# Two of the four block sums of each down unit made by adding transfers instead of VectorE

## The chip, the cores and the metric

The kernel runs on one core of a Trainium2 chip. The metric is device time in microseconds (us). It was run three times; the median is 1215.81 us, the lowest 1213.68 us and the highest 1215.82 us. The profiled execution is a run of its own. The five engines of the core have their own in-order queues: TensorE (PE in the profile), VectorE (DVE), ScalarE (ACT), GpSimd (POOL) and SyncE (SP). They wait for each other through semaphores only. Transfers between DRAM and the on-chip memory are issued from the queues of SP, ACT or POOL and then run beside the engines.

## The reference, cut to what matters

The program is one step of a two-layer decoder on 512 prompt rows and 64 sample rows, 576 in all, with a model width of 1024. Each layer has a mixer and an MLP. The change touches the MLP's second product alone:

```python
def sqrelu_mlp(h, w_up, w_down):
    return jnp.square(jax.nn.relu(h @ w_up)) @ w_down      # w_up 1024 x 4096, w_down 4096 x 1024

for l in range(DEPTH):                                     # 2 layers
    ...mixer...
    hp = hp + sqrelu_mlp(rmsnorm(hp, norm_mlp[l]), mlp_w_up[l], mlp_w_down[l])
    hs = hs + sqrelu_mlp(rmsnorm(hs, norm_mlp[l]), mlp_w_up[l], mlp_w_down[l])
```

All of it is in 32-bit floats.

## The kernel before, in words

**Exactness by splitting.** TensorE is used with a shorter float format. Each operand is therefore split in two: a high half (ScalarE copies it into the short format, `whi` for weights, line 272) and a low half (VectorE subtracts the high half from the original, `wlo`, line 283). A product is three passes: high by high, low activations by high weights, high activations by low weights. A pass cannot start before its half has been made.

**The MLP in rounds.** An MLP has four rounds (`rounds_of`), so the two layers have eight. A round makes eight pieces of the hidden layer (the up part, 384 matmuls of line 328 in a row on the chain) and then the part of the down product that these pieces feed. That down part has four units (`down_unit`, m = 0 to 3). A unit takes a 2 x 2 arrangement of weight blocks and a 2 x 2 arrangement of activation blocks and makes the product with seven block products instead of eight, by the scheme of Winograd and Strassen. The price is sums of blocks. The weight blocks are called a11, a12, a21, a22, each 128 x 512 floats (256 KB). The four sums of weights are s1 = a21 + a22, s2 = s1 + a11, s3 = a21 + a11, s4 = s2 + a12 (the signs are in the data's layout and in the additions to the result). The products use them so:

```python
SOURCE = {"P1": "a11", "P2": "a12", "P4": "a22", "P5": "s1", "P6": "s2", "P7": "s3", "P3": "s4"}
UNIT = ("P1", "P5", "P6", "P2", "P7", "P3", "P4")          # order on TensorE, units m = 1 to 3
FIRST_UNIT = ("P1", "P2", "P3", "P5", "P6", "P4", "P7")    # unit m = 0
```

A unit is 84 matmuls, and its results are added to the rows `h` by VectorE (`to_h`, line 547). The last unit of the last round is left as an ordinary product (`last_unit`), so there are 31 units.

**Loads.** `order` is the list of all weight tiles in the order of use, and `load_to` issues a load of 512 KB for each from SP into a buffer `raw`. A down unit takes two of them: the first holds a11 and a12, the second a21 and a22. There are three `raw` buffers. One more, the spare, serves the second tile of units 1 and 3. It shares its memory (tag `q`) with the tile `q` of the activations, so its load for unit 1 has to wait until the last activation sum of the round has been read out of `q`, which is the second subtraction of line 499 (`alo`).

**Order of the work.** In the MLP the order of VectorE and ScalarE is exactly the order in which the program's lines run (a manual schedule). `ahead_to(n)` prepares weights up to n jobs ahead. Before each of them it looks two jobs further and, by the table `SUMS`, issues the sum that belongs to the job, through `total` (line 257). So sums stand on VectorE's queue some places ahead of the halves that need them, and whatever a sum waits for, all later VectorE work waits for too. The order on SP and POOL is left to the scheduler of the language. POOL does nothing in the down parts.

Of the kernel before, what the change touches and what calls it, by code (L numbers as in the profile page):

```python
# [11 lines left out]
F32 = mybir.dt.float32  # L12
F32R = mybir.dt.float32r
AF = mybir.ActivationFunctionType
ALU = mybir.AluOpType
# [3 lines left out]
P = 128  # L19
# [92 lines left out]
COL = {"mix0": 0, "mlp0": 8, "mix1": 16, "mlp1": 24, "fin": 32, "b_o": 40, "b_qkv": 48, "sink_s": 58}  # L112
NCOL = 59
UNIT = ("P1", "P5", "P6", "P2", "P7", "P3", "P4")
SUMS = {"P1": "s1", "P5": "s2", "P2": "s3", "P6": "s4"}
FIRST_UNIT = ("P1", "P2", "P3", "P5", "P6", "P4", "P7")


# [1 line left out]
def hybrid_step(ctx: ExitStack, tc: tile.TileContext, a, o):  # L120
    nc = tc.nc
# [34 lines left out]
    for c in range(KC):  # L156
# [3 lines left out]
        if c % 2 == 0:  # L160
            raw = wp.tile([P, 512], F32, name="rawf", tag="raw", bufs=3)
# [20 lines left out]
    order = [V[1], Q[0], K[1], Q[1], V[2], K[2], Q[2], V[3], K[3], Q[3], *GV, *G, *U]  # L182
# [6 lines left out]
    def add_pieces(aps):  # L189
        for ap in aps:  # L190
            jobs.extend([("left", len(order)), ("right", len(order))])
            order.append(ap)

    def add_unit(pair, first):
        jobs.extend((n, len(order)) for n in (FIRST_UNIT if first else UNIT))
        order.extend(pair)

    def mlp_order(l, last):
        up, dn = a[f"w_up{l}"], a[f"w_dn{l}"]
        for r in range(32 // FB):  # L200
            add_pieces([up[r * FB + f] for f in range(FB)])
            for m in range(KC // 2):
                if last and r == 32 // FB - 1 and m == KC // 2 - 1:
                    add_pieces([dn[r, m, i] for i in range(2)])
                    continue
                add_unit([dn[r, m, i] for i in range(2)], m == 0)
                if m % 2:
                    spare.append(len(order) - 1)
# [6 lines left out]
    raws, parts, owed, spare_open = [], [], [], [False]  # L215
    used, done, summed = [0], [0], [0]
    sums, sum_pool = {}, [None]
# [5 lines left out]
    def load_to(n):  # L223
        while len(raws) < min(n, len(order)):
            if len(raws) in spare:
                raw = sum_pool[0].tile([P, 1024], F32, name="raw", tag="q", bufs=1)
            else:
                raw = wp.tile([P, 1024], F32, name="raw", tag="raw", bufs=3)
            nc.sync.dma_start(out=raw, in_=order[len(raws)].rearrange("p k c -> p (k c)"))
            raws.append(raw)  # L230

    def load_free():

        while len(raws) < len(order):
            n = len(raws)
            if n in spare:
                free = spare_open[0] and all(i < done[0] for i in spare if i < n)
            else:
                same = [i for i in range(n) if i not in spare]
                free = len(same) < 3 or same[-3] < done[0]  # L240
            if not free:
                break
            load_to(n + 1)

    def blocks_of(i):
        load_to(i + 2)
        return {"a11": raws[i][:, 0:512], "a12": raws[i][:, 512:1024],
                "a21": raws[i + 1][:, 0:512], "a22": raws[i + 1][:, 512:1024]}

    def total(k, i):  # L250

        if (k, i) not in sums:
            b = blocks_of(i)
            x, y = {"s1": ("a21", "a22"), "s2": ("s1", "a11"), "s3": ("a21", "a11"), "s4": ("s2", "a12")}[k]
            x = b[x] if x in b else total(x, i)
            sums[k, i] = sum_pool[0].tile([P, 512], F32, name=k, tag="sum", bufs=4)
            nc.vector.tensor_tensor(out=sums[k, i], in0=x, in1=b[y], op=ALU.add)  # L257
        return sums[k, i]
# [3 lines left out]
    def prepare():  # L262

        n, i = jobs[len(parts)]
        if n in ("left", "right"):
            load_to(i + 1)
            src = raws[i][:, 0:512] if n == "left" else raws[i][:, 512:1024]
        else:
            src = blocks_of(i).get(SOURCE[n])
            src = total(SOURCE[n], i) if src is None else src  # L270
        hi, lo = (wp.tile([P, 512], F32R, name=t, tag=t, bufs=NW_) for t in ("whi", "wlo"))
        nc.scalar.copy(out=hi, in_=src)  # L272
        owed.append((src, hi, lo, n, i))
        parts.append((hi, lo))
# [5 lines left out]
    def split_low(n=1):  # L280
        for _ in range(min(n, len(owed))):
            src, hi, lo, n_, i = owed.pop(0)
            nc.vector.tensor_tensor(out=lo, in0=src, in1=hi.bitcast(F32), op=ALU.subtract)  # L283
            if n_ == "P2":

                total("s4", i)
                total("s3", i)
            if n_ in ("right", "P2", "P4"):
                done[0] = i + (2 if n_ == "P4" else 1)

    def split_to(n):
        while len(parts) < min(n, len(jobs)):
            prepare()
            split_low(len(owed))

    def ahead_to(n):

        n = min(n, len(jobs))
        while len(parts) < n or owed:
            while summed[0] < min(len(parts) + 2, len(jobs)):  # L300
                job, i = jobs[summed[0]]
                k = SUMS.get(job)
                if k:
                    total(k, i)
                summed[0] += 1
            if len(parts) < n:
                prepare()
            split_low()
        load_free()
# [367 lines left out]
    def mixer0(norm, nxt):  # L677
        with tc.tile_pool(name="mx0", bufs=2) as mp:
# [31 lines left out]

            split_high(4)
            split_low(2)
            xs = norm.xs
            cosr, sinr = w("cosr"), w("sinr")
# [692 lines left out]
```

## Time and profile before

| | |
|---|---|
| time of the profiled execution | 1217.04 us |
| its span | 1215.2 us (granted TensorE clock 0.994) |
| median of three runs | 1215.81 us |
| TensorE busy | 1190.1 us, 98% of the span |
| VectorE busy | 869.1 us, 72% |
| ScalarE busy | 576.8 us, 47% |
| GpSimd busy | 156.1 us, 13% |
| read from DRAM | 102.92 MB |

Between the span and the time of the execution lie 1.84 us. A row of the profile's groups reads: line, engine, operation, output<-input, partitions x elements, type, count | busy us, mean ns of one | idle time of the engine ahead of it and what ended it. A row of the chain of waits reads: start in us from the span's start, length in us, what the chain passed through (a DMA, an engine's instruction, or "issue", in which the profile shows no wait). A row of the timeline has start, length from the start of the first to the end of the last, engine, line, operation, operands, shape, count and, in brackets, the idle time before and what ended it. Lines are those of the kernel before.

### The profile page before, as it was taken

To read this page: it belongs to the slowest core of one execution; us is meant where nothing else is said; L and a number is where in the kernel's file an instruction comes from. 1 tells how busy PE (TensorE), PEld (TensorE's weight loads), DVE (VectorE), ACT (ScalarE), POOL (GpSimd) and SP (SyncE) were. 2 spreads that over 40 slices of the span, in tenths; PEclk is the share of its full clock that TensorE was granted. 3 is DMA by queue.
4 is the path that set the end of the run, shared out by engine and by line. 5 is a ranking of instruction groups with operands and counts; after the bars stand their busy time and mean duration, and the time that the engine had idled before them with its cause. 6 is when DMAs were issued, how large, how long until landed. Compare 5 with 4: busy or idle time off the path is not lost.

```text
span 1215.2 us, 22586 instructions
## 1 busy us (share of the span) xinstructions
PE 1190.1 (98%) x9177; PEld 1172.4 (96%) x9177; DVE 869.1 (72%) x1608; ACT 576.8 (47%) x1084; POOL 156.1 (13%) x137
## 2 busy tenths in 40 slices
PE   8999999999999999999999999999999999999996
PEld 8998999999999999999999989999999999999996
DVE  8967685447865875785796768646794795695696
ACT  6333554344443544453465777535453553453452
POOL 3443250110000000000001654120000000000000
PEclk9999999999999999999999999999999999999998
DMA  7244222222232232232223212122223132232222
GB/s 271 104 140 120 78 71 74 85 70 87 88 105 71 84 118 72 73 108 85 86 86 111 70 38 70 36 87 70 83 92 105 52 122 86 72 105 87 76 81 79
DMA packets 38263, 109.42 MB, mean 90 GB/s; under 512 B 4160, under 2 KB 12544, under 8 KB 38144
## 3 DMA queue, kind: packets, MB, share of 16 engines
q1 hardware_dynamic: 37440, 107.36, 28.7%
q8 instruction: 72, 1.18, 0.4%
q10 hardware_dynamic: 720, 0.62, 0.2%
q14 instruction: 31, 0.25, 0.1%
HBM read 102.92 MB, written 6.03 MB: 90 GB/s over the span
## 4 chain that ended last, share of the span: by engine, by line
PE 80%; DVE 11%; DMA 3%; ACT 3%; issue 2%; SPq 0%; DVEq 0%; ACTq 0%
PE acc L328 53%; PE acc L340 8%; PE f L340 3%; PE y L340 3%; PE w L340 3%; PE z L340 3%; DVE wlo L283 3%; DMA raw<-in_w_dn 2%; PE op L1166 1%; PE tpp L1153 1%; DVE alo L499 1%; PE sp L1134 1%; ACT ahi L498 1%; DVE h L547 1%; PE dn L328 1%
## 5 line engine op out<-in xcount | busy, mean ns | idle before, releaser
L328 PE MATMUL acc<-xhi,whi 128*128 128x288 f32 x1520 | 326.0, 296 | 2.6 <-DVE z L1034 2.2
L328 PE MATMUL acc<-xhi,wlo 128*128 128x288 f32 x1520 | 323.6, 294 | 0.0
L328 PE MATMUL acc<-xlo,whi 128*128 128x288 f32 x1520 | 322.5, 294 | 0.0
L283 DVE TENSOR_TENSOR wlo<-raw,whi 128x512 fp32r<-128x512 f32 x321 | 227.7, 722 | 80.9 <-ACT whi L272 79.4
L272 ACT CAST whi<-raw 128x512 fp32r<-128x512 f32 x321 | 191.4, 617 | 143.5 <-PE acc L328 109.5
L328 PEld LDWEIGHTS acc<-xhi,whi 128*128 128x128 f32 x1520 | 242.8, 189 | 4.3 <-issue 3.8
L328 PEld LDWEIGHTS acc<-xhi,wlo 128*128 128x128 f32 x1520 | 243.7, 188 | 0.3
L328 PEld LDWEIGHTS acc<-xlo,whi 128*128 128x128 f32 x1520 | 243.2, 188 | 0.0
L495 ACT ACTIVATE q<-t 128x576 f32<-128x576 f32 x64 | 43.9, 685 | 229.6 <-DVE t L490 229.6
L490 DVE SCALAR_TENSOR_TENSOR t<-acc,rstd 128x576 f32<-128x576 f32 x64 | 48.3, 755 | 82.9 <-PE acc L328 82.7
L272 ACT CAST whi<-s 128x512 fp32r<-128x512 f32 x124 | 73.7, 619 | 65.3 <-DVE s L257 55.8
L283 DVE TENSOR_TENSOR wlo<-s,whi 128x512 fp32r<-128x512 f32 x124 | 83.4, 683 | 10.6 <-ACT whi L272 10.6
L499 DVE TENSOR_TENSOR alo<-q,ahi 128x864 fp32r<-128x864 f32 x64 | 77.1, 1205 | 8.3 <-ACT ahi L498 8.3
L498 ACT CAST ahi<-q 128x864 fp32r<-128x864 f32 x64 | 66.5, 1038 | 13.6 <-DVE q L506 12.6
L340 PE MATMUL acc<-ahi,wlo 128*128 128x288 f32 x340 | 71.3, 298 | 0.6
L340 PE MATMUL acc<-ahi,whi 128*128 128x288 f32 x340 | 71.4, 295 | 0.0
L340 PE MATMUL acc<-alo,whi 128*128 128x288 f32 x340 | 70.3, 295 | 0.0
L257 DVE TENSOR_TENSOR s<-raw 128x512 f32<-128x512 f32 x62 | 42.5, 686 | 19.7 <-DMA raw<-in_w_dn 19.7
L1041 POOL TENSOR_TENSOR kl<-z,kh 64x512 fp32r<-64x512 f32 x4 | 5.5, 1365 | 394.4 <-ACT kh L1038 394.2
L340 PEld LDWEIGHTS acc<-ahi,wlo 128*128 128x128 f32 x340 | 53.6, 188 | 2.5 <-DVE wlo L283 2.5
L340 PEld LDWEIGHTS acc<-ahi,whi 128*128 128x128 f32 x340 | 54.0, 188 | 0.0
L340 PEld LDWEIGHTS acc<-alo,whi 128*128 128x128 f32 x340 | 53.7, 188 | 0.0
(329 smaller groups left out, 2090.5 us busy)
## 6 DMA issues: line engine op xcount, KB each, us to landing
raw<-in_w_up SPq DMA_DIRECT2D x64, 512.0 KB
raw<-in_w_dn SPq DMA_DIRECT2D x64, 512.0 KB
raw<-in_w_in SPq DMA_DIRECT2D x22, 512.0 KB
raw<-in_w_o SPq DMA_DIRECT2D x16, 512.0 KB
raw<-in_w_qkv SPq DMA_DIRECT2D x10, 512.0 KB
h<-in_xT SPq DMA_DIRECT2D x8, 288.0 KB
s<-in_s SPq DMA_DIRECT2D x4, 512.0 KB
out_ret_s<-s SPq DMA_DIRECT2D x4, 512.0 KB
```

What stands on the lines that cost most here:

```text
L257: nc.vector.tensor_tensor(out=sums[k, i], in0=x, in1=b[y], op=ALU.add)
L272: nc.scalar.copy(out=hi, in_=src)
L283: nc.vector.tensor_tensor(out=lo, in0=src, in1=hi.bitcast(F32), op=ALU.subtract)
L328: nc.tensor.matmul(out, lhsT=w_, rhs=x_[:, hf if isinstance(hf, slice) else half(hf)], start=(start and si == 0), stop=(stop and si == 2))
L340: nc.tensor.matmul(out, lhsT=w[wi][:, k * P:(k + 1) * P], rhs=x(k)[xi], start=(start and n == 0), stop=(stop and n == len(steps) - 1), ski ...
L490: nc.vector.scalar_tensor_tensor(out=halves(t), in0=view, scalar=0.0, in1=norm.rv, op0=ALU.max, op1=ALU.mult)
L495: nc.scalar.activation(out=flat(q[:, seg]), in_=t, func=AF.Square)
L498: nc.scalar.copy(out=hi[:, s0 - 1:s1 - 1], in_=q[:, s0:s1])
L499: nc.vector.tensor_tensor(out=lo[:, s0 - 1:s1 - 1], in0=q[:, s0:s1], in1=hi.bitcast(F32)[:, s0 - 1:s1 - 1], op=ALU.subtract)
L547: nc.vector.tensor_tensor(out=row[:, cols_], in0=row[:, cols_], in1=src, op=op)
L1134: nc.tensor.matmul(sp[:, i * 256 + 256 - wd:(i + 1) * 256], lhsT=q[kv][:, n * P:(n + 1) * P], rhs=kst[kv][part][:, lo:lo + wd], start=(par ...
L1153: nc.tensor.transpose(out=tp[:, i * P:(i + 1) * P], in_=s[:, n, hf * P:(hf + 1) * P], identity=ident)
```

## The change

It takes s1 and s3 from VectorE. When `load_to` has issued the load of a unit's second tile (a21, a22), it now issues three more transfers, each of 256 KB:

- from SP, a21 once more from DRAM into a new tile `s3`;
- from POOL, a22 from DRAM, added onto the a21 that lies in the loaded tile, which so becomes s1;
- from POOL, a11 from DRAM, added onto `s3`.

The adds are transfers with `accum_op`: what arrives is added to what lies in the destination. Each waits for the load that fills its destination. s2 and s4 stay on VectorE. The tile `s1` is gone, so the four buffers of tag `sum` now hold three tiles a unit. `SUMS` no longer places s1 and s3; s2 is placed with P5, as before.

```diff
-SUMS = {"P1": "s1", "P5": "s2", "P2": "s3", "P6": "s4"}
+SUMS = {"P5": "s2", "P6": "s4"}
...
+    seconds = set()
+
     def add_unit(pair, first):
         jobs.extend((n, len(order)) for n in (FIRST_UNIT if first else UNIT))
+        seconds.add(len(order) + 1)
         order.extend(pair)
...
-            nc.sync.dma_start(out=raw, in_=order[len(raws)].rearrange("p k c -> p (k c)"))
+            src = order[len(raws)].rearrange("p k c -> p (k c)")
+            nc.sync.dma_start(out=raw, in_=src)
+            if len(raws) in seconds:
+
+                i = len(raws) - 1
+                sums["s3", i] = sum_pool[0].tile([P, 512], F32, name="s3", tag="sum", bufs=4)
+                nc.sync.dma_start(out=sums["s3", i], in_=src[:, 0:512])
+                sums["s1", i] = raw[:, 0:512]
+                nc.gpsimd.dma_start(out=sums["s1", i], in_=src[:, 512:1024], accum_op=ALU.add)
+                nc.gpsimd.dma_start(out=sums["s3", i], in_=order[i].rearrange("p k c -> p (k c)")[:, 0:512],
+                                    accum_op=ALU.add)
             raws.append(raw)
...
     def blocks_of(i):
         load_to(i + 2)
-        return {"a11": raws[i][:, 0:512], "a12": raws[i][:, 512:1024],
-                "a21": raws[i + 1][:, 0:512], "a22": raws[i + 1][:, 512:1024]}
+        return {"a11": raws[i][:, 0:512], "a12": raws[i][:, 512:1024], "a22": raws[i + 1][:, 512:1024]}
 
     def total(k, i):
 
+        b = blocks_of(i)
         if (k, i) not in sums:
-            b = blocks_of(i)
-            x, y = {"s1": ("a21", "a22"), "s2": ("s1", "a11"), "s3": ("a21", "a11"), "s4": ("s2", "a12")}[k]
-            x = b[x] if x in b else total(x, i)
+            x, y = {"s2": ("s1", "a11"), "s4": ("s2", "a12")}[k]
+            x = total(x, i)
...
             if n_ == "P2":
 
                 total("s4", i)
-                total("s3", i)
```

The places where it moves instructions, in the second round of the first layer. First VectorE, where unit 0 ends and unit 1 begins. The second tile of unit 1 is `raw_4755`, the first is `raw_4542` before and `raw_4544` now; `wlo_4801` before and `wlo_4807` now is the low half of its P1; `wlo_4780` before and `wlo_4786` now is the low half of unit 0's P7. Before:

```order
L257 TENSOR_TENSOR s1_4777<-raw_4755 128x512
L283 TENSOR_TENSOR wlo_4780<-s3_4607,whi_4779 128x512
L547 TENSOR_TENSOR h0_74<-h0_74,acc_4696 128x288 x2
L257 TENSOR_TENSOR s2_4798<-s1_4777,raw_4542 128x512
L283 TENSOR_TENSOR wlo_4801<-raw_4542,whi_4800 128x512
L257 TENSOR_TENSOR s4_4804<-s2_4798,raw_4542 128x512
L283 TENSOR_TENSOR wlo_4807<-s1_4777,whi_4806 128x512
```

and now (lines have moved by 4 to 12):

```order
L295 TENSOR_TENSOR wlo_4786<-s3_4480,whi_4785 128x512
L558 TENSOR_TENSOR h0_74<-h0_74,acc_4696 128x288 x2
L269 TENSOR_TENSOR s2_4804<-raw_4755,raw_4544 128x512
L295 TENSOR_TENSOR wlo_4807<-raw_4544,whi_4806 128x512
L269 TENSOR_TENSOR s4_4810<-s2_4804,raw_4544 128x512
L295 TENSOR_TENSOR wlo_4813<-raw_4755,whi_4812 128x512
```

The sum s1 has left the head of this stretch. The first instruction that needs the second tile is now s2, three places further on, and it needs that tile after the add. P1's low half still stands right behind s2.

Second, POOL's queue, which held nothing between the end of the first mixer and the second one. Now, for the same round (`raw_4478` and `s3_4480` belong to unit 0, `raw_4755` and `s3_4757` to unit 1, `raw_4763` and `s3_4765` to unit 2, `raw_4881` and `s3_4883` to unit 3):

```order
L241 DMA s3_4757<-in_w_dn0 128x512
L241 DMA s3_4765<-in_w_dn0 128x512
L240 DMA raw_4755<-in_w_dn0 128x512
L240 DMA raw_4763<-in_w_dn0 128x512
L241 DMA s3_4883<-in_w_dn0 128x512
L240 DMA raw_4881<-in_w_dn0 128x512
```

The scheduler put the adds that make s3 of units 1 and 2 ahead of the add that makes s1 of unit 1.

Third, SP's queue of the same stretch:

```order
L233 DMA raw_4544<-in_w_dn0 128x1024
L238 DMA s3_4757<-in_w_dn0 128x512
L233 DMA raw_4761<-in_w_dn0 128x1024
L238 DMA s3_4765<-in_w_dn0 128x512
L233 DMA raw_4755<-in_w_dn0 128x1024
L233 DMA raw_4763<-in_w_dn0 128x1024
L238 DMA s3_4883<-in_w_dn0 128x512
```

The order of the `raw` loads is as before; the plain loads of `s3` stand between them, that of unit 2 ahead of unit 1's second tile.

## The prediction

> **What bounds the kernel now.** I read the busy time of the engines by stage first. The round's two parts, up and down, in the second round of the first layer:
>
> ```profile
> core 0: us, PE busy (x) PEld busy (x) DVE busy (x) ACT busy (x) POOL busy (x), PEclk, DMA share, GB/s
> 360.00:407.00 47.00, 47.00 (x363) 47.00 (x363) 28.25 (x44) 18.79 (x28) 0.00 (x0) 1.00 0.24 77
> 407.00:455.00 48.00, 47.91 (x361) 47.51 (x360) 40.62 (x76) 23.47 (x43) 0.00 (x0) 1.00 0.34 102
> ```
>
> TensorE is the bound in both parts: in the down part its weight loads leave 0.49 of 48 us idle. VectorE is busy for 85% of that part and idle for the rest, so taking work from it can pay only where TensorE waits for it. I looked for that place in the chain of waits, which is TensorE nearly everywhere, except for one passage in each round. In this round, where unit 0 ends and unit 1 begins:
>
> ```profile
> 411.08 1.37 DVE alo L499
> ...
> 412.47 3.50 DMA raw<-in_w_dn
> ...
> 415.99 0.04 DVE s L257
> 416.03 0.57 issue
> 416.60 0.69 DVE wlo L283
> 417.28 0.73 DVE h L547 x2
> 418.01 0.60 DVE s L257
> 418.61 0.61 DVE wlo L283
> ...
> 419.27 0.79 PE acc L340 x4
> ```
>
> The second tile of unit 1 goes to the spare buffer, which the last activation sum frees at 412.45. The load lands at 415.97. VectorE then makes s1, the low half of unit 0's P7, two additions to h, s2, and at last the low half of unit 1's P1, for which TensorE is waiting. This passage stands in the chain eight times, once a round; the first and the last:
>
> ```profile
> 317.32 3.64 DMA raw<-in_w_dn
> ...
> 1162.21 3.69 DMA raw<-in_w_dn
> ```
>
> How long TensorE waits is in its timeline. Passes of four matmuls start 0.53 us apart when nothing holds them:
>
> ```profile
> 416.70 0.70 PE L340 MATMUL z<-alo,whi 128*128 128x288 f32 x4
> 417.33 0.79 PE L340 MATMUL z<-ahi,wlo 128*128 128x288 f32 x4
> 417.97 0.69 PE L340 MATMUL acc<-ahi,whi 128*128 128x288 f32 x4
> 418.50 0.69 PE L340 MATMUL acc<-alo,whi 128*128 128x288 f32 x4
> 419.27 0.79 PE L340 MATMUL acc<-ahi,wlo 128*128 128x288 f32 x4
> 419.90 0.30 PE L340 MATMUL f<-ahi,whi 128*128 128x288 f32 x1
> ```
>
> From 416.70 to 419.90 there are six passes' starts, five steps, where 2.65 us would do. They took 3.20, so the wait is 0.55 us a round, 4.4 us over eight rounds. That is all that a faster VectorE could win here.
>
> **The change part by part.** *Removed:* 62 sums, s1 and s3 of 31 units:
>
> ```profile
> L257 DVE TENSOR_TENSOR s<-raw 128x512 f32<-128x512 f32 x62 | 42.5, 686 | 19.7 <-DMA raw<-in_w_dn 19.7
> ```
>
> This is 42.5 us of VectorE. Outside the passage above they lie under TensorE's passes, which have no idle time to give back, so I count 0 for them; if TensorE were not the bound, the price of that cover would be at most those 42.5 us.
>
> *Added, issue and bytes:* 31 plain loads from SP and 62 adds from POOL, 256 KB each, 24.4 MB beside 102.92 MB. An issue on SP takes 0.33 us (row below), so about four more a round are 1.3 us of that queue in some 95 us. POOL was idle in the down part (0.00 in the windows). In the window 407 to 455 some 4.9 MB moved (48 us by 102 GB/s) at a DMA share of 0.34. The adds bring 3.1 MB more from DRAM, and if reading the destination costs as much again as its 2.1 MB, the share becomes 0.34 x 10.1 / 4.9 = 0.70. The engines of the DMA are not full, so I count 0, and put crowding into the range.
>
> *Moved:* the wait. VectorE's first instruction that needs unit 1's second tile is now s2, and it needs it after the add. The low half of unit 0's P7 and the two additions now stand ahead of that wait, which is good. But the low half of unit 1's P1 still stands behind s2. So let X be the time from the landing of the load to the landing of the add. TensorE's pass then starts at 415.97 + X + 0.60 (s2) + 0.69 (low half) + 0.02, and before it started at 419.27. The change of the round is 415.97 + X + 1.31 - 419.27 = X - 1.99 us, and never less than -0.55. Queued behind s2 on VectorE are P1's low half, s4 and the low half of s1; on ScalarE the high half of s1 waits for the add itself (0.62 us a cast), is done at X + 0.62 and so before P1's last pass ends at X + 1.84. One wait a round, at P1, is the whole of it as long as the later units are in time.
>
> Are they? Of the 16 waits in that group's row eight are the passage above and eight are s1 of unit 0, in the up part. These are s1 and s2 of unit 0, then the issues of the second tiles of units 1 and 2 and of unit 3, and s2 of units 2 and 3:
>
> ```profile
> 392.23 0.69 DVE L257 TENSOR_TENSOR s<-raw 128x512 f32<-128x512 f32 x1 [1.18 <-DMA raw<-in_w_dn]
> 401.36 1.41 DVE L257 TENSOR_TENSOR s<-s,raw 128x512 f32<-128x512 f32 x2
> ...
> 412.47 1.74 SPq L229 DMA_DIRECT2D raw<-in_w_dn  x2
> 425.75 0.33 SPq L229 DMA_DIRECT2D raw<-in_w_dn  x1
> 426.37 0.68 DVE L257 TENSOR_TENSOR s<-s,raw 128x512 f32<-128x512 f32 x1
> 435.18 0.68 DVE L257 TENSOR_TENSOR s<-s,raw 128x512 f32<-128x512 f32 x1
> ```
>
> Unit 0: landed 392.2, s2 at 401.36, room for X up to 9.1. Unit 2: issued 413.88, landed 3.6 later at 417.5, s2 at 426.37, room for X up to 8.9. Unit 3: landed about 429.3, s2 at 435.18, room 5.9, and VectorE's half made next is some passes early, so I let a second wait begin at X = 7. On POOL the add for unit 1's s1 stands behind those for s3 of units 1 and 2. Their loads wait for buffers that VectorE frees ahead of the activations' last sum, so they are through by 412 and POOL is free at 415.97. On SP the plain load of s3 for unit 2 stands ahead of unit 1's second tile, but that tile waits for 412.45 anyway.
>
> *The price X.* The trace has no add and no transfer from POOL. Nearest rows: the load itself, a small plain transfer at the end, SP's issue, and POOL's own work on 128 x 512 elements:
>
> ```profile
> SPq L1392 <- DMA out_y<-y: 1.8, 2, 1.4
> 1211.99 0.33 SPq L646 DMA_DIRECT2D out_y<-y x1
> L229 SPq DMA_DIRECT2D raw<-in_w_dn x4: 327/328/328, 412.5 to 425.8; - x4
> L815 POOL TENSOR_TENSOR qd<-qT,cst 128x512 f32<-128x512 f32 x4 | 6.1, 1532 | 0.2
> ```
>
> The last line of output, 144 KB, is issued at 1211.99, its issue takes 0.33, and SP then waits at most 1.4: about 1.75 us. The 512 KB load takes 3.50. A straight line between the two gives 1.75 + 1.75 x 112 / 368 = 2.28 us for a plain 256 KB, the low end. For the value I take that the add reads 256 KB from DRAM and 256 KB of destination, as much as the 512 KB load moves: 3.50, less SP's issue of 0.33, plus POOL's making of the transfer, for which I take an estimate midway between SP's 0.33 and POOL's 1.53 for a pass over 128 x 512: 0.93. So X = 3.50 - 0.33 + 0.93 = 4.10. The high end: two transfers in a row, one reading and one writing, 2 x 3.50, and POOL at 1.53, 8.5 us.
>
> The page "DMA: Bandwidth & Descriptors" of the Trainium skill (section "Anatomy of one DMA — SWDGE (gpsimd) path") prices a transfer from GpSimd at 2.0 us plus its bytes over 436 GB/s, which is an estimate of 2.6 us here, and the sum would be about 5 us slower. For 512 KB it gives 3.2 where the trace's load took 3.50, so it is a little low. The page "Collectives: The Full Stack" of the Trainium skill (section "The bandwidth ceiling: the fold count and why AG ≠ RS ≠ AR") says that an adding transfer has two source reads and halves the rate; with that the estimate is 3.2 us, and the sum about 10 us slower. No run here shows an add yet.
>
> *The sum:* 8 x (4.10 - 1.99) = 8 x 2.11 = 16.9 us. Made against the profiled execution: 1217.04 + 16.9 = 1233.9. That execution lies 1.23 us above the median of the runs, 1215.81, so for the runs I predict 1215.81 + 16.9, which is 1233 us.
>
> **The rivals.** *Late twice.* If X reaches 7, s2 of unit 3 is late too, and each further us costs 2 us a round. At X = 8.5 the price is 8 x (6.51 + 1.5) = 64 us, 1280. For it speaks that building, reading, adding and writing may not overlap; against it that the DMA engines are mostly idle and a 512 KB load takes only 3.5.
>
> *A short add.* Reading the destination costs nothing beside the read from DRAM, and POOL issues as fast as SP: X between 2.28 and 2.8, 8 x 0.29 to 8 x 0.8, 2 to 6 us, 1218 to 1222. The straight line speaks for it; that POOL has no row as short as 0.33 for 128 rows of data speaks against it. The first of the two pages names this case.
>
> *Not slower: the wait at P1 of unit 1 goes.* The mechanism is the one place above: when X is at most 1.99 the load and the add together are no later than load and sums were, and at X of 1.44 or less all 0.55 us a round are won: 4.4 us, 1211. It decides at X = 1.99. For it speaks the 1.75 us of the small output; against it that this was a plain transfer of 144 KB.
>
> **How the numbers follow.** The likeliest case, one wait a round with X from 3 to 7, has 0.65; its own range is 8 to 40 us, 1224 to 1256. Late twice 0.13, the short add 0.13, not slower 0.07; 0.02 is for what I do not see. A measurement of this kernel can tell about 0.2% (2.4 us) from no change. Slower by more: 0.65 + 0.13 + 0.10 of the short add + 0.01 = 0.89. Within: 0.03 of the short add, 0.02 of not slower and 0.01, 0.06. Faster: 0.05. The range reaches from 1219, which holds most of the short add, to 1270, which is X = 7.7 with the second wait (8 x (5.71 + 0.7) = 51 us, 1267). Outside lie not slower, a little of the short add and half of late twice, together about 0.18.
>
> **What would show it right or wrong.** Right: in the chain, after each of eight loads into the spare buffer, a second DMA into `raw` that ends X later, then s2, then P1's low half, then TensorE; TensorE idle there for X - 1.44 us a round, 2.7 us at X = 4.1; no other wait in the down part; VectorE about 42 us less busy, TensorE's busy time unchanged; DMA share in the down part between 0.56 and 0.70. The steps can fail singly: X is read off directly; a wait at P5, P7 or in unit 3 would mean that the other adds are late or that POOL's order matters; a longer load ahead of the add would mean crowding. The prediction is wrong in kind if VectorE's sums turn out to have held TensorE elsewhere, so that rounds get shorter.

## The result, and the profile after

The changed kernel takes 1253.38 us (median; lowest 1252.72, highest 1253.8) beside 1215.07 us for the kernel before. The ratio is 1.0299, with a 95% interval of 1.0284 to 1.0314, so about 36 us are lost. The profiled executions agree: 1252.72 against 1217.04 us, with spans of 1250.6 and 1215.2 us, 35.4 us apart. The two medians lie a little further apart, 38.3 us; below I go by 36. The prediction had 16.9 us and a time of 1233 us. The sign, the place and the one wait a round are as predicted; the loss is twice as large.

The page of the changed kernel first: the busy time of the engines, what was read from DRAM, the group of POOL's adds into `raw`, and the last row of the issues (31 issues of 256 KB each, with the median us from issue to landing at the end):

```profile
PE 1199.7 (96%) x9177; PEld 1183.2 (95%) x9177; DVE 836.8 (67%) x1546; ACT 578.3 (46%) x1084; POOL 210.0 (17%) x199
HBM read 127.30 MB, written 6.03 MB: 107 GB/s over the span
L240 POOL DMA_DIRECT2D raw<-in_w_dn x31 | 26.8, 865 | 455.9 <-DMA raw<-in_w_dn 385.0
raw<-in_w_dn POOLq DMA_DIRECT2D x31, 256.0 KB, 4.5
```

VectorE is 32 us less busy (869.1 before; the prediction had about 42), POOL 54 us more (156.1 before: 62 issues at 0.87 us). TensorE is 9.6 us *more* busy (1190.1 before) with the same 9177 matmuls. That last number was not predicted, and most of the loss that the sum lacks will turn out to hang on it.

The chain of waits of the changed kernel at the predicted place, in the second round (start, length, what):

```profile
418.30 3.51 DMA raw<-in_w_dn
...
421.87 0.48 issue
...
422.37 4.37 DMA raw<-in_w_dn
...
426.75 0.69 DVE s L269
427.45 0.61 DVE wlo L295
...
428.10 0.80 PE acc L351 x4
428.90 2.67 PE f L351 x12
431.58 2.04 PE acc L351 x12
433.61 1.60 PE y L351 x12
```

Up to 428.10 this is the predicted chain: the load into the spare, which the last activation sum releases, a second DMA into the same tile, s2, the low half of P1, TensorE. The load lands at 418.30 + 3.51 = 421.81 and the add at 422.37 + 4.37 = 426.74, so X is 4.93 us. Read in the same way in the six rounds in which the chain shows both landings, X is 4.84 to 5.35 us, 5.0 in the mean. The choice had been 4.10.

Behind 428.10 something happens that the prediction does not have. Twelve matmuls take 1.57 to 1.60 us when nothing holds them, as in the last row. P5 (`f`) takes 2.67 here and P6 (`acc`) 2.04: 1.5 us more for the same work. TensorE's timeline shows that no wait stands in it:

```profile
424.12 0.69 PE L351 MATMUL acc<-alo,whi 128*128 128x288 f32 x4
428.10 0.80 PE L351 MATMUL acc<-ahi,wlo 128*128 128x288 f32 x4 [3.29 <-DVE wlo L295]
428.74 0.91 PE L351 MATMUL f<-ahi,whi 128*128 128x288 f32 x4
429.45 1.16 PE L351 MATMUL f<-alo,whi 128*128 128x288 f32 x4
430.41 1.16 PE L351 MATMUL f<-ahi,wlo 128*128 128x288 f32 x4
431.37 1.16 PE L351 MATMUL acc<-ahi,whi 128*128 128x288 f32 x4
432.33 0.74 PE L351 MATMUL acc<-alo,whi 128*128 128x288 f32 x4
```

TensorE idles for 3.29 us, and then passes follow each other at 0.96 us instead of 0.53, until about 432. It is the granted clock (PEclk), the share of full speed at which TensorE runs. The same stretch in windows of 3.41 us, laid so that they begin and end where the granted clock changes (columns: stretch, its length, busy time and instructions of each engine, granted clock, DMA share, GB/s):

```profile
core 0: us, PE busy (x) PEld busy (x) DVE busy (x) ACT busy (x) POOL busy (x), PEclk, DMA share, GB/s
422.16:425.58 3.42, 2.65 (x21) 2.41 (x19) 0.87 (x3) 0.00 (x0) 1.67 (x2) 1.00 0.72 177
425.58:428.99 3.41, 0.89 (x6) 0.89 (x7) 2.23 (x4) 1.81 (x4) 0.06 (x1) 1.00 0.61 81
428.99:432.40 3.41, 3.41 (x17) 3.41 (x16) 3.41 (x8) 2.43 (x5) 0.00 (x0) 0.50 0.25 78
432.40:435.82 3.42, 3.42 (x27) 3.42 (x27) 3.42 (x8) 1.54 (x3) 0.86 (x1) 0.99 0.90 188
```

In the second window TensorE is busy for 0.89 of 3.41 us. In the third it is busy throughout, at a clock of 0.50, and has 17 matmuls where the fourth has 27. The clock record in the trace of the changed kernel has such a stretch in each of the eight rounds, 3.41 us long in five of them and 6.83 in three; the kernel before has none in its MLPs.

For the whole of the down part, in the same window of time as in the prediction, and TensorE's waits over the run (total, times, longest):

```profile
407.00:455.00 48.00, 44.71 (x327) 44.47 (x326) 35.05 (x65) 22.11 (x40) 5.19 (x6) 0.96 0.58 138
PE acc L351 <- DVE wlo L295: 28.2, 8, 4.4
```

The one new wait is the one predicted, 28.2 / 8 = 3.5 us a round. The next in that list come to 2.4 us or less over the whole run, and none of them is at a matmul of a down unit (L351).

### The profile page after: what moved, and what is told of

Read it like the earlier page. It is cut to its first block, busy times and chain, and to the rows that moved or that the text cites. A ratio compares the mean times of both kernels' runs of the same rounds, so it can differ in the third digit from the quotient of the medians.

```text
span 1250.6 us, 22819 instructions
## 1 busy us (share of the span) xinstructions
PE 1199.7 (96%) x9177; PEld 1183.2 (95%) x9177; DVE 836.8 (67%) x1546; ACT 578.3 (46%) x1084; POOL 210.0 (17%) x199
## 3 DMA queue, kind: packets, MB, share of 16 engines
HBM read 127.30 MB, written 6.03 MB: 107 GB/s over the span
## 4 chain that ended last, share of the span: by engine, by line
PE 80%; DVE 9%; DMA 5%; ACT 3%; issue 2%; SPq 0%; DVEq 0%; POOLq 0%; ACTq 0%
PE acc L339 52%; PE acc L351 9%; DMA raw<-in_w_dn 4%; PE f L351 4%; PE y L351 3%; PE w L351 3%; PE z L351 3%; DVE wlo L295 2%; ACT s L1104 1%; PE tpp L1164 1%; PE op L1177 1%; PE sp L1145 1%; DVE alo L510 1%; PE dn L339 1%; ACT ahi L509 1%
## 5 line engine op out<-in xcount | busy, mean ns | idle before, releaser
L295 DVE TENSOR_TENSOR wlo<-raw,whi 128x512 fp32r<-128x512 f32 x352 | 248.8, 721 | 93.9 <-ACT whi L284 92.0
L284 ACT CAST whi<-raw 128x512 fp32r<-128x512 f32 x352 | 211.7, 619 | 182.7 <-PE acc L339 111.6
L240 POOL DMA_DIRECT2D raw<-in_w_dn x31 | 26.8, 865 | 455.9 <-DMA raw<-in_w_dn 385.0
L351 PE MATMUL acc<-ahi,wlo 128*128 128x288 f32 x340 | 74.6, 310 | 28.2 <-DVE wlo L295 28.2
L351 PEld LDWEIGHTS acc<-ahi,wlo 128*128 128x128 f32 x340 | 56.3, 198 | 30.1 <-DVE wlo L295 30.1
L295 DVE TENSOR_TENSOR wlo<-s,whi 128x512 fp32r<-128x512 f32 x93 | 63.2, 686 | 19.9 <-ACT whi L284 19.9
L351 PE MATMUL acc<-ahi,whi 128*128 128x288 f32 x340 | 72.4, 302 | 0.0
L351 PE MATMUL acc<-alo,whi 128*128 128x288 f32 x340 | 71.4, 299 | 0.0
L241 POOL DMA_DIRECT2D s<-in_w_dn x31 | 27.0, 870 | 228.1 <-DMA s<-in_w_dn 110.4
L284 ACT CAST whi<-s 128x512 fp32r<-128x512 f32 x93 | 56.9, 620 | 17.9 <-DVE wlo L295 11.6
L351 PEld LDWEIGHTS acc<-ahi,whi 128*128 128x128 f32 x340 | 56.0, 196 | 0.0
L351 PEld LDWEIGHTS acc<-alo,whi 128*128 128x128 f32 x340 | 54.9, 192 | 0.0
```

What stands on the lines that cost most here:

```text
L240: nc.gpsimd.dma_start(out=sums["s1", i], in_=src[:, 512:1024], accum_op=ALU.add)
L241: nc.gpsimd.dma_start(out=sums["s3", i], in_=order[i].rearrange("p k c -> p (k c)")[:, 0:512], accum_op=ALU.add)
L351: nc.tensor.matmul(out, lhsT=w[wi][:, k * P:(k + 1) * P], rhs=x(k)[xi], start=(start and n == 0), stop=(stop and n == len(steps) - 1), ski ...
```

## The experiments

The theory after the result: (a) the add for s1 of unit 1 is late by X - 1.99 us a round, with X of 4.9 and not 4.10, about 23 us; (b) the wait of some 3.3 us that this makes takes half of TensorE's clock for the next 3.41 us, about 1.5 us a round, 12 us. Rivals: the cost is spread over the extra transfers (crowding, or POOL's order); and the slow passes are not caused by the wait. Ratios below are against the kernel before on the same chip, with the 95% interval.

**1. The adds for s1 alone.** The plain load of `s3` stays; its sum is on VectorE again (its place in `SUMS` and the call in the low halves, both not shown, are back too).

```diff
-                nc.gpsimd.dma_start(out=sums["s3", i], in_=order[i].rearrange("p k c -> p (k c)")[:, 0:512],
-                                    accum_op=ALU.add)
+                loaded[i] = sums.pop(("s3", i))
...
+        if k == "s3" and (k, i) not in sums:
+            sums[k, i] = loaded[i]
+            nc.vector.tensor_tensor(out=loaded[i], in0=loaded[i], in1=b["a11"], op=ALU.add)
```

> The add for s1 stays a transfer in all 31 units; s3's tile is still loaded plainly, but its sum is made on VectorE again. Theory (the change costs what unit 1's s1 costs at P1's low half, and TensorE runs at half clock after that wait): as the changed kernel, X still about 4.9 us and 1250 to 1255 us. Rival (crowding: the 31 adds for s3 hold up s1's on GpSimd or in the DMA engines): X falls by 0.5 us or more, and the time to 1240 to 1248.

Measured: 1251.76 us, 1.028 (1.0255 to 1.0306). In its chain the load into the spare and the add in the third round:

```profile
519.30 3.58 DMA raw<-in_w_dn
...
523.44 4.57 DMA raw<-in_w_dn
...
528.04 0.69 DVE s L271
```

X is 528.01 - 522.88 = 5.1 us here, and 4.6 to 5.1 in the other rounds that show it, and the clock record has half clock in seven of the eight rounds. Without the 31 adds for s3 the add for s1 is nearly as slow as with them (4.9 us in the mean). Neither they nor their place on POOL hold it up.

**2. The adds for s3 alone.** s1 is made by VectorE, in place on the loaded block.

```diff
-SUMS = {"P5": "s2", "P6": "s4"}
+SUMS = {"P1": "s1", "P5": "s2", "P6": "s4"}
...
-                sums["s1", i] = raw[:, 0:512]
-                nc.gpsimd.dma_start(out=sums["s1", i], in_=src[:, 512:1024], accum_op=ALU.add)
...
+        if k == "s1" and (k, i) not in sums:
+            sums[k, i] = raws[i + 1][:, 0:512]
+            nc.vector.tensor_tensor(out=sums[k, i], in0=sums[k, i], in1=b["a22"], op=ALU.add)
```

> s1 is made on VectorE again (in place, on the loaded block), s3 stays a plain load and an add. Theory: the place is as in the kernel before, so 1213 to 1218 us, with TensorE's wait of about 0.5 us a round and no half clock. Rival (crowding, each extra transfer costs): half of the loss stays, about 1234.

Measured: 1215.29 us, 0.9985 (0.997 to 1.0001), no difference that can be told. The chain at the place reads as that of the kernel before:

```profile
413.90 3.55 DMA raw<-in_w_dn
...
420.09 0.61 DVE wlo L296
...
420.75 0.79 PE acc L352 x4
```

From the start of the load to TensorE's pass are 6.85 us; before they were 419.27 - 412.47 = 6.80. The adds for s3 are hidden, and the 21 us that VectorE no longer spends on them buy nothing.

**3. All adds but those of unit 1.** The lines below are the difference from the changed kernel's loads; the table `SUMS` and the sums themselves are as in the kernel before, and a sum that a transfer has made is not made again.

```diff
+                if m == 1:
+                    ones.add(len(order) - 1)
...
-            if len(raws) in seconds:
+            if len(raws) in seconds - ones:
```

> Only unit 1 of each round has s1 and s3 on VectorE as before; the other 23 units keep both adds. Theory: the whole loss goes with 8 of 31 units, 1212 to 1218 us. Rival (the cost is spread over the adds): 23/31 of 38 us stay, about 1244.

Measured: 1217.83 us, 1.0000 (0.9986 to 1.0014). With 46 of the 62 adds still made, the loss is gone. It sits in unit 1 of each round, whose second tile goes to the spare while TensorE is about to need it.

**4. s2 made later, so that P1's low half no longer stands behind it.** It is now made when s4 asks for it.

```diff
-SUMS = {"P5": "s2", "P6": "s4"}
+SUMS = {"P6": "s4"}
```

> Both adds stay; s2 is asked for with P6 and no longer two products ahead, so that on VectorE the low half of unit 1's P1 stands ahead of s2. Theory: P1 no longer waits; the wait moves to the high half of P5, which is made from s1: 415.97 + 4.92 + 0.62 (cast) = 421.5 against 419.90 in the kernel before, +1.6 us a round or 13 us, 1229, if TensorE keeps its clock through a wait of about 2.2 us; about 1241 if its clock halves again. Rival (the wait at P1 is not the cause): 1250 or more.

Measured: 1243.38 us, 1.0205 (1.018 to 1.0229), 25 us slower than before: the second of the two figures. The first two passes of P5 in TensorE's timeline:

```profile
424.69 1.03 PE L351 MATMUL f<-ahi,whi 128*128 128x288 f32 x4 [2.07 <-ACT whi L284]
425.51 1.16 PE L351 MATMUL f<-alo,whi 128*128 128x288 f32 x4
```

P1 now runs through, and the wait stands at P5's high half, as worked out. But 2.07 us of idle time are enough for half clock: the clock record has it in six of the eight rounds.

**5. Filling the wait.** The changed kernel, with 24 matmuls that nobody reads in the place where TensorE waits. The arithmetic of the lateness is untouched; only the idle time goes.

```diff
         for n, (k, (wi, xi)) in enumerate(steps):
+            if warm_ is not None and n == 2 * len(ks_):       # unit 1, P1
+                for j in range(24):
+                    nc.tensor.matmul(warm_, lhsT=w[0][:, (j % 4) * P:(j % 4 + 1) * P], rhs=x(j % 4)[0], start=True,
+                                     stop=True, skip_group_check=True)
```

> As the changed kernel, with 24 matmuls of 128x288 (about 0.13 us each, 3.2 us) on TensorE in unit 1, after the second pass of P1, into a half of the accumulator tile that this unit leaves unused: they fill the wait and change no output. Theory (late by 2.9 us a round, and half clock after the wait for about 1.5 us a round more): the 23 us stay, the 12 go, and no half clock shows in the down part: 1238 to 1244 us. Rival (the clock falls for another reason, or what I take for it is only the wait): 1252 us or more.

Measured: 1239.76 us, 1.0201 (1.0181 to 1.0221). The chain of this kernel:

```profile
421.90 3.20 PE acc L353 x24
425.09 0.66 PE acc L355 x4
425.76 1.59 PE f L355 x12
427.35 1.59 PE acc L355 x12
```

P5 and P6 take 1.59 us again, and the clock record has no half clock in any down part. The kernel does more work than the changed one and is about 12 us faster (1.0299 - 1.0201 = 0.0098, of 1215; by the two intervals, 8 to 16). So part (b) of the theory is shown, with its size. What is left, 24 us, is part (a): 8 x (5.0 - 1.99) = 24.1. In the five rounds of this run whose chain shows both landings X is 4.8 to 5.9 us, 5.1 in the mean.

**6 and 7. What the add itself costs.** The transfer for s1 copies its block and does not add; first from POOL as in the changed kernel, then from SP.

```diff
-                nc.gpsimd.dma_start(out=sums["s1", i], in_=src[:, 512:1024], accum_op=ALU.add)
+                nc.gpsimd.dma_start(out=sums["s1", i], in_=src[:, 512:1024])     # run 6
+                nc.sync.dma_start(out=sums["s1", i], in_=src[:, 512:1024])       # run 7
```

> The transfer for s1 is left on GpSimd's queue with the same block and size but copies and does not add, so s1 is wrong in all 31 units and so is what follows from it; its wait for the load stays. If adding itself costs (the destination is read): X = 0.5 + 0.87 + 1.95 = 3.3 us by the straight line between plain transfers, TensorE waits 1.9 us, 1226 to 1240 us (few or many half-clock windows). If a transfer from GpSimd costs this whatever it does: X 4.6 to 4.9, 1248 to 1254 us.

> The same copy, issued on SP behind the load and not on GpSimd (s1 is again the copied block and no sum). If GpSimd's issue (0.5 us to start and 0.87 us to make) is the part of X that a plain transfer does not have: X falls to about 2.3 to 2.8 us, TensorE waits 0.9 to 1.4 us, no half clock in the down part, 1218 to 1224 us. If the second step over the memory is what costs: X 3.5 or more, 1232 us or more.

Measured: run 6 1239.77 us, 1.0206 (1.0186 to 1.0225); run 7 1231.76 us, 1.0139 (1.0117 to 1.0162). The chain of run 6 in the second round, and POOL's issues of it (ns, least, median and most):

```profile
415.82 3.29 DMA raw<-in_w_dn
...
419.70 3.20 DMA raw<-in_w_dn
...
422.92 0.69 DVE s L269
L240 POOL DMA_DIRECT2D raw<-in_w_dn x31: 554/559/600, 297.2 to 1186.8; - x31
```

and the chain of run 7 in the fifth:

```profile
883.17 3.50 DMA raw<-in_w_dn
...
886.69 3.41 DMA raw<-in_w_dn
```

In run 6 X is 422.90 - 419.11 = 3.8 us here and 3.9 in the mean of the seven rounds that show it; in run 7 it is 3.4 here and in the mean (3.0 to 3.7; in four rounds the chain does not show the copy's landing, and X is read up to the start of s2, which needs it). So X of 5.0 is, as measured at this place, 3.4 for a plain copy of 256 KB from SP behind a load, 0.5 more for POOL's queue, and 1.1 more for adding, of which 0.3 are POOL's longer issue (0.87 against 0.56). Both expectations were missed in size. POOL's copy cost 0.6 us more than its first case says, and SP's copy was near its second case with no second step over the memory in it: a plain 256 KB took as long as the 512 KB load of 3.50 us just ahead of it. The straight line down to the small output, 2.28 us, was wrong for this place.

The copy of run 7 is not alone, though. This is the window of its 3.41 us (columns as above):

```profile
886.70:890.10 3.40, 2.99 (x23) 2.75 (x21) 1.20 (x3) 0.27 (x1) 0.00 (x0) 1.00 0.58 204
```

At 204 GB/s some 0.69 MB moved in it, of which the copy is 0.26; the rest is mostly the load of unit 2's second tile, which SP issues just behind that of unit 1. The single DMA packets in the traces show who shares the engines with whom. Run 7's copy has its first packet 1.0 us after the load's landing, and in the three rounds in which they can be told apart 150 to 210 KB of other data move beside it. The adds of the changed kernel have their first packet 2.1 us after the landing (2.8 in the last round), when unit 2's load is over or nearly so, and at most 60 KB move beside them; run 6 has 1.8 to 1.9 us and at most 32 KB. So crowding is no large part of X for the adds, but it may be one for run 7's copy: what such a copy takes by itself, and with it the true share of POOL's queue, stays open.

Half clock came in six rounds of run 6 and four of run 7. With X - 1.99 for each of eight rounds and 1.5 us for each round with half clock, run 6 comes to 15 + 9 = 24 us and run 7 to 11 + 6 = 17; measured are 25 and 17. For the changed kernel the same sum is 24 + 12 = 36, as measured.

**8. The kernel before, with s1 made only when s2 asks for it.** This is the floor of the prediction, the 0.55 us a round, tried without any transfer.

```diff
-SUMS = {"P1": "s1", "P5": "s2", "P2": "s3", "P6": "s4"}
+SUMS = {"P5": "s2", "P2": "s3", "P6": "s4"}
```

> The kernel before, with all sums on VectorE, but s1 no longer made two products ahead: it is made when s2 asks for it, so that in unit 1 the low half of P7 and two additions stand ahead of the wait for the load and not behind s1. Theory: P1's low half is done at 415.97 + 0.02 + 0.60 + 0.60 + 0.69 = 417.9, ahead of the 418.7 at which TensorE wants it: the 0.55 us a round go, 1211 us, 0.9964 of before. Rival (the wait is taken up by the next thing, P7's or P5's halves): no change.

Measured: 1214.51 us, 0.9991 (0.9979 to 1.0004): no difference that can be told, and not the 4.4 us. Its chain at the place:

```profile
414.74 0.38 ACT z L570
415.12 0.55 ACT whi L272
...
415.69 0.39 DVE wlo L283
...
416.30 0.81 DVE h L547 x2
...
419.10 0.79 PE acc L340 x4
```

The load has left the chain. In its place stand ScalarE's copy of P6, the halves of P7 and two additions, which I had assumed to be over by then, and P1's last pass begins 0.90 us after the one ahead of it. The rival was right: the next thing is almost as late.

**9 and 10. s1 and s2 made when P5 and P6 ask for them,** in the kernel before, and in run 2's kernel.

```diff
-SUMS = {"P1": "s1", "P5": "s2", "P2": "s3", "P6": "s4"}
+SUMS = {"P6": "s2", "P2": "s3"}                                # run 9
...
-SUMS = {"P1": "s1", "P5": "s2", "P6": "s4"}
+SUMS = {"P6": "s2"}                                            # run 10
```

> The kernel before, all sums on VectorE, with s1 and s2 made when P5 and P6 ask for them, so that the low half of unit 1's P1 stands ahead of both. It no longer waits for the second tile; what does is the high half of P5, ready at about 416.6 + 0.6 + 0.6 = 417.8, ahead of its 419.3. Theory (in the kernel before 0.55 us a round are lost at this place, and s1 made late left 0.2 of them): the place costs nothing, 1211 to 1213 us, 0.9964 to 0.998 of before. Rival (TensorE's waits there are paid back elsewhere, or are smaller than the steps of its passes show): within 0.1% of before.

> As the run that makes s3 alone by transfer, with s1 (in place on VectorE) and s2 made when P5 and P6 ask for them. Theory: the place costs nothing and the adds for s3 are all hidden, so as the kernel before with s1 and s2 late, 1211 to 1213 us. Rival (taking 21 us of sums from VectorE is worth something by itself): 2 us or more below that run.

Measured: run 9 1220.1 us, 1.003 (1.0016 to 1.0044), a little slower than before and outside both of its cases; run 10 1216.99 us, 0.9999 (0.9988 to 1.001). Run 10's theory missed too, and its rival came out in number: it is 3.1 us below run 9. TensorE's longest waits in run 9:

```profile
PE z L340 <- ACT z L592: 3.0, 8, 0.4
...
PE acc L340 <- ACT y L583: 2.4, 3, 1.8
```

The wait at P1 is gone, and TensorE waits for ScalarE's copies of results instead. One of those waits, 1.8 us long, was followed by half clock. Run 10 has no such long wait and no half clock in a down part, and from one up part to the next its rounds are 95.22 us long and run 9's, where no half clock falls, 95.30: 0.6 us over eight rounds. So the wait and its clock in one round of run 9, about 1.8 and 1.5 us, are enough for the 3.1 us, and it is not shown that the 21 us taken from VectorE are worth anything by themselves. No order of the sums that I tried beats the kernel before.

**11. How much idle time takes the clock.** As run 5, with 12 filling matmuls.

```diff
-                for j in range(24):
+                for j in range(12):
```

> As the run with 24 filling matmuls, but 12 of them (1.6 us), so that TensorE still idles for about 1.7 us a round. In the runs so far windows of 3.41 us in which TensorE idled for 1.8 us or less kept their clock, and those with 1.9 us or more were followed by one at half clock. By that bound: no half clock in the down part, and the time of the run with 24, about 1240 us. If a shorter wait is enough to halve the clock: 1246 to 1254 us.

Measured: 1243.52 us, 1.0219 (1.0198 to 1.0241), between the two figures. The waits left are longer than planned in single rounds:

```profile
PE acc L355 <- DVE wlo L295: 14.7, 8, 2.6
```

That is 1.84 us in the mean, but not even: seven rounds kept their clock, among them one with a wait of 2.6 us that was split over two windows; in one, with 2.4 us, it halved.

**12. Run 4 with its wait filled,** by 15 matmuls after P1's third pass.

```diff
+        if warm_ is not None:                                  # unit 1, P1
+            for j in range(15):
+                nc.tensor.matmul(warm_, lhsT=w[0][:, (j % 4) * P:(j % 4 + 1) * P], rhs=x(j % 4)[0], start=True,
+                                 stop=True, skip_group_check=True)
```

> Both adds, s2 asked for with P6 as in the run before that did this, and 15 filling matmuls (2.0 us) on TensorE after the third pass of unit 1's P1, where that kernel waits for P5's high half. They change no output. Theory (that kernel's 25 us are about 13 from P5 being late and about 12 from half clock after its wait of 2.1 us): the 13 stay, 1227 to 1232 us, no half clock in the down part. Rival (the clock costs little there, and what is late is more than P5): 1238 us or more.

Measured: 1235.81 us, 1.015 (1.0133 to 1.0167), between the two figures: 18 us slower than before and 6.7 us faster than run 4. No half clock shows in its down parts. Two of its passes:

```profile
423.71 0.79 PE L351 MATMUL f<-ahi,whi 128*128 128x288 f32 x4
...
425.11 0.80 PE L351 MATMUL f<-ahi,wlo 128*128 128x288 f32 x4
```

The direction is the theory's, the sizes are not quite: half clock cost run 4 about 7 us (six rounds of 1.1), and the lateness is 18 and not 13. In this kernel P5's low half is late as well: from its first to its last pass stand 1.40 us where 1.06 would do, because s2 and s4 now come ahead of that half on VectorE. Eight times 0.34 on top of 13 make 16; the last 2 us were not located.

## Why the prediction was right in kind and short in size

*Place and mechanism: right.* One wait a round, where unit 0 ends and unit 1 begins, through s2 and the low half of P1. Shown by runs 1 to 3: the loss stays with s1's adds alone and goes when unit 1 of each round, 8 of 31 units, is taken out.

*The rule, change of a round = X - 1.99: right.* With the clock kept (run 5) the loss is 24 us, and 8 x (5.0 - 1.99) is 24.1.

*The term X = 3.50 - 0.33 + 0.93 = 4.10: too small by 0.9, 7 us in the sum.* In the round shown, POOL starts 0.56 us after the landing and issues for 0.87, 1.43 in place of 0.93; the transfer then takes 3.50 in place of 3.17. I had made POOL's part from one duration, its issue; the time that its queue needs to start at all is a second one. The low bound fell too: the small output at the end is no measure for 256 KB between other transfers. The two estimates that the prediction worked out from the Trainium skill, 2.6 us ("DMA: Bandwidth & Descriptors", section "Anatomy of one DMA — SWDGE (gpsimd) path") and 3.2 us ("Collectives: The Full Stack", section "The bandwidth ceiling: the fold count and why AG ≠ RS ≠ AR"), lie below every X that the chains show for a transfer from POOL (3.45 us and more, in run 6), and the trace decides. What the second of these sections of the Trainium skill says is said of the reduce step of a collective.

*A term that was missing: TensorE's clock, 12 us.* "TensorE's busy time unchanged" is the step that failed most: it rose from 1190.1 to 1199.7 us. The sum counted the idle time of TensorE and took the work behind it as unchanged. It does not hang on the mis-sized X: with 4.10 the wait would still have been 2.66 us, and waits of 2.1 us (run 4) and of 2.3 us in the mean (run 6) halved the clock in six of eight rounds. The sign was there in the kernel before, in the second layer's mixer. This is TensorE's wait there, and the two windows of 3.41 us around it:

```profile
657.50 0.50 PE L328 MATMUL acc<-xhi,whi 128*128 128x288 f32 x2 [2.23 <-DVE z L1034]
655.60:659.00 3.40, 1.50 (x11) 1.53 (x12) 2.95 (x5) 1.62 (x4) 0.11 (x1) 1.00 0.09 12
659.00:662.40 3.40, 3.40 (x17) 3.40 (x16) 0.00 (x0) 2.18 (x4) 3.28 (x3) 0.50 0.49 151
```

A wait of 2.23 us, and behind it a window at 0.50. Anyone who asks what a new wait of 2 to 3 us costs can read it off there.

*Luck.* The measured time lies within 1219 to 1270, but that range was drawn for other reasons: its upper end stands for a second wait at X = 7.7, and neither the wait nor such an X came. The clock was not among the reasons.

*Hidden work: right.* The sums taken from VectorE away from the wait bring nothing that can be told (31 of them in run 2, 46 in run 3). That VectorE is 32 us less busy and not 42 is in part a matter of reading: neighbouring rows overlap by 0.08 us (415.99 + 0.69 against the next start, 416.60, in the kernel before), 5 us over 62 sums. The rest was not located; it changes nothing in the sum. The DMA share in 407 to 455 is 0.58, within 0.56 to 0.70, and the extra adds crowd nothing that shows (run 1; the load ahead of the add is 3.51 us long, 3.50 before). DRAM reads are 127.30 MB, 24.4 more, as counted. No second wait appears in units 0, 2 or 3.

*The floor of -0.55 us a round: not to be had so.* Runs 8 to 10 show that other work stands just behind the load at this place.

## What to carry to other kernels

A transfer that adds saves VectorE its pass, but here the sum was there 5 us after the loaded block had landed and not 0.7 us; use it only for sums whose block lands that much ahead, and leave to VectorE those that are on the path (here 8 of 31 units). Even so it gained nothing here (run 3), because VectorE was not what the kernel waited for. When a change makes TensorE wait, count the wait and then look in the profile for the clock after waits of the same length; the work behind the wait may cost half as much again as the lateness (here 12 us beside 24). A wait that can't be avoided may be worth filling with matmuls that nobody reads: here that gave back a third of the loss.

## What the hardware showed that was not expected

**The clock goes by windows, and here some two idle microseconds in one were enough.** In all the traces of this case the granted clock changes on a grid of 3.41 us that keeps its phase through an execution. I laid TensorE's idle time on each trace's grid, without the ends of the executions. All 41 windows at full clock with 1.89 us of idle time or more were followed by one at half clock. Of the windows with 1.85 or less only one was (1.78 us, run 9; a second, of 1.79 us, lies at the end of that execution), apart from six in the second layer's mixer, at 769 to 780 us, in six of the experiments: these follow windows without idle time. What stands there is a row of narrow matmuls, 64 columns by 64, of 4.2 us and more; here its first four in run 10:

```profile
765.61 0.34 PE L1246 MATMUL opS<-pTS,cv 128*64 128x64 f32 x4
```

In each of the 14 traces the grid cuts that row in its own way. In the six with half clock 2.96 us or more of it fell into one window, in the eight others at most 2.78. So not every matmul that the profile shows as busy seems to count as work for the clock. An estimate from the rows fits: four matmuls of 288 columns take 0.53 us, so 64 columns would need 0.03 us, but these start 0.066 us apart (the next four begin at 765.88), which leaves over half of such a window, 1.9 us, unused. No run was made to test it.

So the same wait costs its clock or not by where it falls: 2.07 us inside one window did in run 4, 2.6 us split over two did not in run 11. The page "TensorE: Matmul & The Clock Gate" of the Trainium skill (section "HAM oscillation — how this bites in real kernels") gives as the rule that TensorE should have no idle gap above about 3.4 us. The window's length and the half rate agree with the trace; the gap does not, since one of 2.07 us sufficed.

**The price of an adding transfer of 256 KB from POOL:** 0.5 us until POOL starts, 0.87 us for its issue (0.56 for the same transfer as a copy), 4.5 us from the start of the issue to the landing (3.3 as a copy), and 5.0 us from the landing of the load that it waits for; its first packet moves 2.1 us after that landing.

**Half the bytes did not take half the time at this place:** 256 KB copied from SP took 3.4 us behind a 512 KB load that took 3.50. Another load ran beside the copy, so this is no price of a copy by itself.
